# First gate on TensorE, sines on GpSimd, softmax division on ScalarE: one change to a two-layer network kernel

## The chip, the core and the metric

The kernel runs on one core of one Trainium2 chip. The metric is the device time of one launch in microseconds (us). The kernel before takes 1743.57 us (median of three runs, 1743.54 to 1747.07).

The engines are called as in the profile: PE is TensorE, PEld its weight loads, DVE is VectorE, ACT is ScalarE, POOL is GpSimd, SP is SyncE, which here issues every DMA. Each engine runs its own list of instructions in order and waits on semaphores of the others.

## The reference

A sequence of 256 tokens with 1024 channels goes through four mixers (latent attention "MLA", a state space mixer "S5", a gated linear recurrence, block attention) and MLPs. Each layer is modulated by a vector `c`: `silu(c) @ w + b` is cut in three 1024-wide thirds, shift, scale and gate. Only the start of the network is touched by the change:

```
def modulation(cs, w, b):
    m = cs @ w + b
    shift, scale, gate = jnp.split(m, 3, axis=-1)

z = h @ w_in                                   # 1024 -> 256 + 128 + 64
cq  = rms_norm(z[..., :256], q_norm)
ckv = rms_norm(z[..., 256:384], kv_norm)
k_pe = apply_rope(z[..., 384:], cos, sin)
q  = cq @ w_qb                                 # 8 heads of 128 + 64
kv = ckv @ w_kvb                               # 8 heads of 128 + 128
p = softmax(where(causal, (qn kn^T + qp k_pe^T) * scale, -1e30))
o = (p @ v) @ w_o
```

The S5 mixer also needs tables of powers of its complex decay (products of sines and cosines of `li * dt * 2^e`), which do not depend on the tokens and are built early.

## The kernel before, in words

All big weights come from one list of 512 KB units, `UNITS`, made by `plan()`. SP loads them in that order into 7 raw buffers. Unit kinds: `w` is a weight that ACT copies to a rounded high part (`wh`, L454) and DVE (`wl`, L460) or POOL (L458) subtracts to a low part, both into a ring of 11 slots; `p` is an MLA weight used as it is, in a slot of the ring that has not been needed yet (`early`); `m` is a modulation unit, 128 columns of a third, for which DVE multiplies the unit with `silu(c)` and sums along the row (one SCALAR_TENSOR_TENSOR of 128x1024 and a short read of the sum, L508). `run(maxn)` takes the next units of the list in order wherever it is called; what it emits stands on DVE, ACT and POOL at that place of the program. A raw buffer is free, and the load seven units further on can start, when the unit's instruction has read it.

Order of the work up to the first MLP, as the code writes it:

- setup: `silu(c)`, decay powers on POOL, then the sines on DVE (`sincos`, L894 to L903), the rotary tables by POOL copies (L975 to L984) and PE transposes (L989).
- `mla`: eight pairs of modulation units (shift and scale of the first layer), each followed by the modulation of 128 channels of the transposed input and the PE product with `mla_in`; then the squares of the latents on ACT (L1071), the power -1/2 on POOL (`rpow`, L635), the normalised latents, their transposes on PE (`turn_z`, L1098), the keys (`kvk`), values (`kvv`) and first query pair (`q_pair`).
- `heads`: eight heads in a software pipeline of letters. S is the scores on PE, B the maximum on DVE, E the exponentials on ACT, N the reciprocal and the division by the sum on DVE (L1210), T the transposes on PE (L1024) with an ACT copy (L1025), A the product with the values; `q` makes the next query pair, a digit calls `run` with that many units, `t` issues background work (the four stores of the recurrence tables, `tab_d`, L1334, which wait for POOL).
- Inside the heads, `run` passes modulation units to DVE: the rest of the second modulation and the eight units of the first layer's gate (`mod02`). When the gate's sums are done, `modfin` is set: `mod_finish` turns the column into rows with 16 PE instructions against the identity (L392 with `gcol`), and while it is pending inside the heads no further modulation unit is taken.
- `mla_o` boundary: output projection in two halves of tokens; for each half a layer norm on DVE (`ln_part`, L651 to L666, with `rpow` on POOL), transposes on PE, the modulated transposed input `z` (L623) and its split `xh`, `xl` (L590).
- MLP 0: the first weights (`mlp0.f`) are used in two passes, one for each half of the tokens; their results leave the banks by a DVE copy (L848), one for each pass, and PE transposes them.

From the second of these two copies on, the two kernels issue the same instructions in the same order on every engine.

Of the kernel before, what the change touches and what calls it, by code (L numbers as in the profile page):

```python
# [38 lines left out]
HEADS0 = "T2 S0 B0 1 A2 E0 N0 t q t 1"  # L39
# [3 lines left out]
ROT = 0  # L43
G0 = 1
GSTEP = 2.0
ROT_T = 21.5
ROT_U = 6.0
# [41 lines left out]
MODS_AT = 8  # L89
# [7 lines left out]
def plan():  # L97
# [4 lines left out]
    m = _mod(1, 0) + _mod(1, 1) + _mod(0, 2)  # L102
# [23 lines left out]
def _unit(inp, kind, tag, k, out):  # L126
# [6 lines left out]
    if kind == "m":  # L133
        i, third = int(tag[3]), int(tag[4])
        nm, l = _MOD[i]
        o = 1024 * third + 128 * k
        out[:] = inp[nm + "_w"][l][:, o:o + 128].T
        return
# [62 lines left out]
def _cols_spec():  # L201
    s = [("dsk", lambda i: i["ssm_d"][0])]
# [112 lines left out]
class Model:  # L315
    def __init__(self, ctx, tc, ws, cols, rows, x, pos, inv, rel, sp, sbc, sgb, out):
# [9 lines left out]
        slot = lambda j: sb.tile([128, 1024], F32, name="early%d" % j, tag="w%s%d" % ("hl"[j % 2], RING - 1 - j // 2))  # L326
        self.pt = {u: slot(6 + j) for j, u in enumerate(PUNITS)}
        self.early = [slot(j) for j in range(6)]
        self.rt, self.nop, self.opdone = [], 0, set()
        self.XH, self.XL = T("xh", [128, 8, 256], F32R), T("xl", [128, 8, 256], F32R)  # L330
# [16 lines left out]
        self.mhalf = T("mhalf", [128, 4])  # L347
        self.lri = T("lri", [128, 8], I32)
# [16 lines left out]
        self.fill = 0  # L365

# [56 lines left out]
    def run(self, look=LOOK, maxn=99, mods=2):  # L423
        n = 0
        while self.nproc < len(UNITS) and n < maxn:
# [13 lines left out]
            if u[0] == "w":  # L439
# [6 lines left out]
                if own is None and s >= RING - 3 and self.early:  # L446
                    break
# [50 lines left out]
    def mod_unit(self, u, raw):  # L498
        nc, tag, k = self.nc, u[1], u[2]
        i, third = int(tag[3]), int(tag[4])  # L500
        if k == 0:
            self.mod_finish()
# [12 lines left out]
        if k == 7:  # L515
            if third < 2:
                nc.vector.tensor_tensor(self.mcol[i][third], self.msum, self.col("modb%d" % i, 8 * third, 8), op=OP.add)
                self.mods.add(tag)
            else:
                nc.vector.tensor_tensor(self.gcol, self.msum, self.col("modb%d" % i, 16, 8), op=OP.add)  # L520
                nc.vector.tensor_scalar(self.gcol, self.gcol, 1.0, None, op0=OP.add)
                self.modfin = [tag, 3]
# [365 lines left out]
    def sincos(self, s, c, ang, t1, t2):  # L888
        nc = self.nc
        tau = 2.0 * math.pi  # L890
# [3 lines left out]
        nc.vector.tensor_scalar(t1, ang, 1.0 / tau, MAGIC, op0=OP.mult, op1=OP.add)  # L894
        nc.vector.tensor_scalar(t1, t1, -MAGIC, None, op0=OP.add)
        nc.vector.scalar_tensor_tensor(t2, t1, -c1, ang, op0=OP.mult, op1=OP.add)
        nc.vector.scalar_tensor_tensor(t2, t1, -c2, t2, op0=OP.mult, op1=OP.add)
        nc.vector.scalar_tensor_tensor(t2, t1, -c3, t2, op0=OP.mult, op1=OP.add)
        nc.vector.tensor_scalar(t2, t2, 3.1415925, -3.1415925, op0=OP.min, op1=OP.max)
        nc.scalar.activation(s, t2, func=AF.Sin)  # L900
        nc.scalar.activation(t1, t2, func=AF.Sin, scale=0.5)
        nc.vector.scalar_tensor_tensor(t1, t1, -2.0, t1, op0=OP.mult, op1=OP.mult)
        nc.vector.tensor_scalar(c, t1, 1.0, None, op0=OP.add)  # L903
# [21 lines left out]
    def setup(self):  # L925
# [3 lines left out]
        spt = self.Z[1][:, 1664:1664 + NSP]  # L929
        inv = self.Z[1][:, 1600:1632]  # L930
# [12 lines left out]
        V.memset(self.mhalf, -0.5)  # L943
        jp = self.Z[0][:, 0:128]
# [12 lines left out]
        self.rel(*cb)  # L957
        self.ssm_decay(spt, pi)
        while self.nproc < 2:
            self.step()  # L960
        V.tensor_copy(self.identb, self.ident)
        V.tensor_copy(self.maskb, self.mask)
        posf = self.stat(2)
        V.tensor_copy(posf, posi)
        n = 64 + 7 * 32
        a, t1, t2 = (self.Z[1][:, n * i:n * i + n] for i in range(3))
        sc = self.Z[1][:, 3 * n:5 * n].rearrange("p (e a) -> p e a", e=2)
        for h in range(2):
            V.tensor_scalar(a[:, 32 * h:32 * h + 32], inv, posf[:, h:h + 1], None, op0=OP.mult)
        for e in range(7):  # L970
            V.tensor_scalar(a[:, 64 + 32 * e:96 + 32 * e], self.sw[2], float(1 << (e + 1)) if e else 1.0, None, op0=OP.mult)
        self.sincos(sc[:, 0], sc[:, 1], a, t1, t2)
        self.tok = self.sb.tile([128, 2, 2, 32], F32, name="tok")
        for e in range(2):
            G.tensor_copy(self.tok[:, e], sc[:, 1 - e, 0:64].rearrange("p (h f) -> p h f", h=2))  # L975
        CT, ST = self.B2, self.BR
        for h in range(2):
            for j in range(4):
                o = slice(128 * h + 32 * j, 128 * h + 32 * j + 32)
                G.tensor_copy(CT[:, o], self.tok[:, 0, h])  # L980
                if j % 2 == 0:
                    G.tensor_scalar(ST[:, o], self.tok[:, 1, h], -1.0, None, op0=OP.mult)
                else:
                    G.tensor_copy(ST[:, o], self.tok[:, 1, h])  # L984
        self.ssm_powers(sc[:, 1, 64:], sc[:, 0, 64:])
# [54 lines left out]
    def mla(self):  # L1040
# [4 lines left out]
        gen = self.ssm_inputs()  # L1045
        next(gen)
        xb = [self.pair_transposes(self.X, 2 * i) for i in range(4)]
        zb = [self.bank(), self.bank()]
        for k in range(8):
# [13 lines left out]
            if k % 2:  # L1063
                self.done(u)
                self.rel(xb[k // 2])
        ZT = self.B2
# [9 lines left out]
        next(gen)  # L1076
        for half in range(2):
            z, o = zb[half], ZT[:, 512 * half:512 * half + 512]
            c, s = self.tok[:, 0, half], self.tok[:, 1, half]
# [14 lines left out]
        for j in (2, 0, 1, 3):  # L1094
# [926 lines left out]
```

## Time and profile before

| quantity | value |
|---|---|
| median of three runs | 1743.57 us |
| profiled execution, its own time | 1742.75 us |
| its span, first to last instruction | 1740.9 us |
| mean granted TensorE clock | 0.956 |
| PE busy | 1602.5 us (92%) |
| DVE busy | 1157.7 us (67%) |
| ACT busy | 833.7 us (48%) |
| POOL busy | 508.8 us (29%) |

The profile shows one execution of the program. The terms of the sum are taken from it and set against its own time. [...] `fp32r` in a shape is the rounded type of the split weights; the `mla` products are plain fp32, for which the trace shows two loads and two MATMUL rows for one product.

### The profile page before, as it was taken

Reading aid. Unit: us, or ns where it says so; the run is one execution under the profiler, and the core shown is the slowest. Engines: PE = TensorE matmul, PEld = TensorE weight load, DVE = VectorE, ACT = ScalarE, POOL = GpSimd, SP = SyncE. Lnnn points to the kernel's source line nnn. Section 1 sums busy time; section 2 is a strip of 40 time slices with the busy share of each in tenths; the row PEclk is TensorE's granted clock in tenths of the full one; section 3 lists DMA queues with packets and bytes.
Section 4 is the critical chain, followed back from the end, with each engine's and each line's share of the span. In section 5 each row is a group of like instructions: output and inputs, shape, how many; then the busy total and the mean of one; then the engine's idle time right before and its main releaser. Section 6 shows DMA issues by size and latency. Waiting matters only on the chain. (4 is left out here: it accounts for less than half of the span.)

```text
span 1740.9 us, 25278 instructions
## 1 busy us (share of the span) xinstructions
PE 1602.5 (92%) x9690; PEld 1417.2 (81%) x9690; DVE 1157.7 (67%) x1480; ACT 833.7 (48%) x1252; POOL 508.8 (29%) x557
## 2 busy tenths in 40 slices
PE   4778999998789999999999759999999999999998
PEld 2557798887677899789998747999899999779997
DVE  6688986578978655776556787555656554765553
ACT  2343656555345655354445735444544443754441
POOL 8945699608848100100004441000000001230000
PEclk9869999898889999999999879999999999999999
DMA  9477678767556666466554336565455664536640
GB/s 365 172 279 256 226 248 281 273 243 263 220 170 222 239 229 212 152 219 225 176 181 134 118 121 217 176 239 173 137 188 214 213 211 133 182 133 207 214 149 25
DMA packets 106588, 349.64 MB, mean 201 GB/s; under 512 B 12385, under 2 KB 22753, under 8 KB 106466
## 3 DMA queue, kind: packets, MB, share of 16 engines
q1 hardware_dynamic: 106466, 348.02, 57.7%
q8 instruction: 76, 1.25, 0.3%
q14 instruction: 46, 0.38, 0.1%
HBM read 338.40 MB, written 9.57 MB: 200 GB/s over the span
## 5 line engine op out<-in xcount | busy, mean ns | idle before, releaser
L460 DVE TENSOR_TENSOR wl<-raw,wh 128x1024 fp32r<-128x1024 f32 x445 | 562.7, 1298 | 193.1 <-ACT wh L454 191.7
L454 ACT ACTIVATE wh<-raw 128x1024 fp32r<-128x1024 f32 x484 | 490.3, 1051 | 275.1 <-PE bank L392 140.9
L392 PE MATMUL bank<-xh,wh 128*128 128x256 f32 x1728 | 490.1, 284 | 0.0
L392 PE MATMUL bank<-xh,wl 128*128 128x256 f32 x1728 | 489.7, 283 | 0.0
L392 PE MATMUL bank<-xl,wh 128*128 128x256 f32 x1728 | 489.1, 283 | 0.0
L392 PEld LDWEIGHTS bank<-xh,wh 128*128 128x128 f32 x1728 | 330.6, 191 | 2.4 <-issue 0.2
L392 PEld LDWEIGHTS bank<-xl,wh 128*128 128x128 f32 x1728 | 330.5, 191 | 2.1
L392 PEld LDWEIGHTS bank<-xh,wl 128*128 128x128 f32 x1728 | 330.5, 191 | 0.0
L392 PE MATMUL bank<-wh,hh 128*128 128x512 f32 x736 | 297.4, 404 | 24.8 <-ACT hh L1827 23.8
L392 PE MATMUL bank<-wl,hh 128*128 128x512 f32 x736 | 294.5, 400 | 2.8 <-POOL wl L458 2.8
L392 PE MATMUL bank<-wh,hl 128*128 128x512 f32 x736 | 244.8, 398 | 4.2 <-DVE hl L590 2.0
L635 POOL TENSOR_TENSOR st<-st,mhalf 128x1 f32<-128x1 f32 (+1 forms) x33 | 21.9, 664 | 694.8 <-DVE st L643 608.1
L458 POOL TENSOR_TENSOR wl<-raw,wh 128x256 fp32r<-128x256 f32 x156 | 156.7, 1037 | 138.0 <-ACT wh L454 129.8
L392 PEld LDWEIGHTS bank<-wh,hh 128*128 128x128 f32 x736 | 142.0, 193 | 55.9 <-ACT hh L1827 25.3
L392 PEld LDWEIGHTS bank<-wh,hl 128*128 128x128 f32 x736 | 141.1, 192 | 37.5 <-DVE hl L590 2.9
L392 PEld LDWEIGHTS bank<-wl,hh 128*128 128x128 f32 x736 | 142.2, 193 | 33.1 <-POOL wl L458 5.0
L508 DVE SCALAR_TENSOR_TENSOR junk<-raw,cs 128x1024 bf16<-128x1024 f32 x96 | 138.0, 1437 | 18.3 <-DMA raw<-in_ws_dram 17.1
L392 PE MATMUL bank<-wl,xh 128*128 128x512 f32 x320 | 126.6, 396 | 1.9 <-DVE wl L460 1.0
L392 PE MATMUL bank<-wh,xh 128*128 128x512 f32 x320 | 127.4, 398 | 0.7 <-ACT wh L454 0.7
L590 DVE TENSOR_TENSOR hl<-z,hh 128x512 fp32r<-128x512 f32 x72 | 52.5, 731 | 95.5 <-ACT hh L589 95.3
L392 PE MATMUL bank<-wh,xl 128*128 128x512 f32 x320 | 102.0, 396 | 6.5 <-DVE xl L590 6.4
L589 ACT ACTIVATE hh<-z 128x512 fp32r<-128x512 f32 x72 | 45.5, 632 | 116.4 <-DVE z L875 104.4
(389 smaller groups left out, 1807.2 us busy)
## 6 DMA issues: line engine op xcount, KB each, us to landing
raw<-in_ws_dram SPq DMA_DIRECT2D x580, 512.0 KB
early<-in_ws_dram SPq DMA_DIRECT2D x10, 512.0 KB
grow<-in_rows_dram SPq DMA_DIRECT2D x9, 512.0 KB
brow<-in_rows_dram SPq DMA_DIRECT2D x6, 512.0 KB
ophh<-ops_d SPq DMA_DIRECT2D x6, 512.0 KB
ophl<-ops_d SPq DMA_DIRECT2D x6, 512.0 KB
gate<-in_rows_dram SPq DMA_DIRECT2D x5, 512.0 KB
tab_d<-early SPq DMA_DIRECT2D x4, 512.0 KB
```

The source lines that it names most:

```text
L392: self.nc.tensor.matmul(out, l, r, start=start, stop=stop)
L454: self.nc.scalar.activation(self.Hs[s], raw, func=AF.Copy)
L458: self.nc.gpsimd.tensor_tensor(self.Ls[s][:, w], raw[:, w], self.f32(self.Hs[s])[:, w], op=OP.subtract)
L460: self.nc.vector.tensor_tensor(self.Ls[s], raw, self.f32(self.Hs[s]), op=OP.subtract)
L508: nc.vector.scalar_tensor_tensor(self.junk, raw, 1.0, self.cs, op0=OP.mult, op1=OP.mult, accum_out=total)
L589: self.nc.scalar.activation(hdst, src, func=AF.Copy)
L590: self.nc.vector.tensor_tensor(ldst, src, self.f32(hdst), op=OP.subtract)
L635: self.nc.gpsimd.tensor_tensor(r, v, self.mhalf[:, 0:n], op=OP.pow)
```

## The change

Six things are done.

1. The eight units of the first gate are stored by rows and multiplied on PE: for each unit, eight 128x128 blocks are loaded as weights and one column of `silu(c)` is streamed (`pe_unit`). In the list they come before the second modulation's units.
2. The sines are made by POOL and two ACT lookups; the rotary tables by ACT copies. The first five steps of the first recurrence table (`rotations`) now stand on POOL ahead of the `rpow` of the latents, the decay powers (`ssm_powers`) and the rest behind it.
3. The division by the softmax sum is an ACT copy with a scale. The recurrence tables are stored after the heads.
4. Modulation units `m[0:5]` and `m[5]` of the second modulation are handled before the heads, the other ten come between the units of `mla_o`.
5. The small decay tables (`ssm_tables`) are turned and stored in the first layer norm of the boundary.
6. The first seven units of `MODS0` move from ahead of `mlp0.f[3]` to behind `mlp0.f[7]`.

```diff
+HEADS0 = "T2 S0 B0 A2 E0 1 N0 q 1"
-HEADS0 = "T2 S0 B0 1 A2 E0 N0 t q t 1"
...
-    for k, (a, b) in enumerate(((0, 0), (0, 2), (2, 4), (4, 24))):
-        o += [("p", "qb", k)] + m[a:b]
-    o += _w("mla_o", 8)
+    m, g, w = _mod(1, 0) + _mod(1, 1), _mod(0, 2), _w("mla_o", 8)
+    o += g[:4] + m[:5] + [("p", "qb", 0)] + g[4:] + m[5:9] + [("p", "qb", k) for k in (1, 2, 3)]
+    for k in range(8):
+        o += [w[k]] + m[9 + k:10 + k]
     m = _ffn_order("mlp0", N_FF, 8, False)
-    o += m[:3] + MODS0[:MODS_PRE] + _weave(m[3:], MODS0[MODS_PRE:], MODS_AT)
+    o += m[:8] + MODS0[:MODS_PRE] + _weave(m[8:], MODS0[MODS_PRE:], MODS_AT)
...
+    def pe_unit(self, tag, k, raw):
+        if k == 0:
+            self.pbk = self.bank()
+        for j in range(8):
+            self.mm(self.pbk[:, j:j + 1], raw[:, 128 * j:128 * j + 128], self.cst[:, k:k + 1],
+                    k == 0 and j == 0, k == 7 and j == 7)
...
-        nc.vector.scalar_tensor_tensor(t2, t1, -c1, ang, op0=OP.mult, op1=OP.add)
...
+        for x in (c1, c2, c3):
+            G.tensor_scalar(t2, t1, -x, None, op0=OP.mult)
+            G.tensor_tensor(ang, ang, t2, op=OP.add)
...
         r = self.rpow(ss, 4)
-        next(gen)
+        self.rotations(0, range(5, 6))
+        self.rotations(1, range(6))
+        self.ssm_powers()
+        self.run(maxn=4, mods=4)
...
+        turn_z((2, 0, 1))
...
-                nc.vector.tensor_scalar(P[h % 3][:, w], P[h % 3][:, w], rc[:, i:i + 1], None, op0=OP.mult)
+                if bias is None:
+                    nc.scalar.activation(P[h % 3][:, w], P[h % 3][:, w], func=AF.Copy, scale=rc[:, i:i + 1])
```

Three places show what this does to the order. The first is PE between the last `mla_in` product and the first query pair; before, the transposes (L1098), keys (`early_74`), values (`early_75`), the small table (L1316) and the queries (`early_76`) follow one another.

```order
L1098 MATMUL bank_125<-ident,b2row 128x128
L1098 MATMUL bank_126<-ident,b2row 128x128
L392 MATMUL bank_127<-gate,early_74 128x256 x2
L392 MATMUL bank_128<-gate,early_74 128x256 x2
L392 MATMUL bank_129<-gate,early_74 128x256 x2
L392 MATMUL bank_130<-gate,early_74 128x256 x2
L392 MATMUL bank_131<-early_75,gate 128x512
L392 MATMUL bank_124<-early_75,gate 128x512
L392 MATMUL bank_125<-early_75,gate 128x512
L392 MATMUL bank_126<-early_75,gate 128x512
L1316 MATMUL bank_127<-ident,grow 128x128 x2
L392 MATMUL bank_128<-gate,early_76 128x256 x4
```

The same stretch after, from the third gate unit on; a row with `cst,raw` is one gate unit.

```order
L401 MATMUL bank_125<-cst,raw_67 128x1 x8
L401 MATMUL bank_125<-cst,raw_68 128x1 x8
L401 MATMUL bank_128<-gate,early_74 128x256 x2
L401 MATMUL bank_124<-gate,early_74 128x256 x2
L401 MATMUL bank_129<-gate,early_74 128x256 x2
L401 MATMUL bank_130<-gate,early_74 128x256 x2
L1157 MATMUL bank_126<-ident,b2row 128x128
L1157 MATMUL bank_127<-ident,b2row 128x128
L401 MATMUL bank_125<-cst,raw_67 128x1 x8
L401 MATMUL bank_131<-early_75,gate 128x512
L401 MATMUL bank_128<-early_75,gate 128x512
L401 MATMUL bank_124<-early_75,gate 128x512
```

One gate unit stands ahead of the transposes, three between them and the keys, one between keys and values and three between values and queries; the small table is gone from here.

The second place is DVE behind the eight heads. Before, from the last but one `hl` (the low part of a head's output) on: only splits (L460), the three modulation columns and, at the end, two modulation units (L508) stand ahead of the layer norm (L651).

```order
L590 TENSOR_TENSOR hl_89<-bank_128,hh_88 128x256
L460 TENSOR_TENSOR wl_55_848<-raw_66,wh_55_847 128x1024
L1005 SCALAR_TENSOR_TENSOR scol<-mc_112,cols 128x8
L1006 SCALAR_TENSOR_TENSOR bcol<-mc_112,cols 128x8
L1007 TENSOR_TENSOR bcol<-bcol,mc_111 128x8
L460 TENSOR_TENSOR wl_56_866<-raw_67,wh_56_865 128x1024
L460 TENSOR_TENSOR wl_57_871<-raw_68,wh_57_870 128x1024
L460 TENSOR_TENSOR wl_58_924<-raw_69,wh_58_923 128x1024
L460 TENSOR_TENSOR wl_59_929<-raw_63,wh_59_928 128x1024
L460 TENSOR_TENSOR wl_60_934<-raw_64,wh_60_933 128x1024
L508 SCALAR_TENSOR_TENSOR junk,msum<-raw_65,cs 128x1024
L508 SCALAR_TENSOR_TENSOR junk,msum<-raw_66,cs 128x1024
```

After, a part of the same stretch, where the units (L520) and the splits (L469) alternate.

```order
L520 SCALAR_TENSOR_TENSOR junk,msum<-raw_67,cs 128x1024
L469 TENSOR_TENSOR wl_43_854<-raw_68,wh_43_853 128x1024
L520 SCALAR_TENSOR_TENSOR junk,msum<-raw_69,cs 128x1024
L469 TENSOR_TENSOR wl_45_861<-raw_63,wh_45_860 128x1024
L520 SCALAR_TENSOR_TENSOR junk,msum<-raw_64,cs 128x1024
L469 TENSOR_TENSOR wl_47_868<-raw_65,wh_47_867 128x1024
L520 SCALAR_TENSOR_TENSOR junk,msum<-raw_66,cs 128x1024
L469 TENSOR_TENSOR wl_49_875<-raw_67,wh_49_874 128x1024
```

Behind the last `hl` there are now ten units and eleven splits ahead of the layer norm; inside the heads there is neither.

The third place is DVE between the two copies of MLP 0. Before, five units stood ahead of the first `z` of the boundary (L623), and behind the first copy came splits at once.

```order
L508 SCALAR_TENSOR_TENSOR junk,msum<-raw_64,cs 128x1024
L623 TENSOR_SCALAR z_100<-bank_128,scol,bcol 128x128 x4
...
L848 COPY z_98<-bank_125 128x512
L460 TENSOR_TENSOR wl_55_848<-raw_63,wh_55_847 128x1024
L460 TENSOR_TENSOR wl_56_866<-raw_64,wh_56_865 128x1024
```

After, seven units stand between the first copy (L880) and the same splits.

```order
L880 COPY z_96<-bank_125 128x512
L520 SCALAR_TENSOR_TENSOR junk,msum<-raw_63,cs 128x1024
L520 SCALAR_TENSOR_TENSOR junk,msum<-raw_64,cs 128x1024
L520 SCALAR_TENSOR_TENSOR junk,msum<-raw_65,cs 128x1024
L520 SCALAR_TENSOR_TENSOR junk,msum<-raw_66,cs 128x1024
L520 SCALAR_TENSOR_TENSOR junk,msum<-raw_67,cs 128x1024
L520 SCALAR_TENSOR_TENSOR junk,msum<-raw_68,cs 128x1024
L520 SCALAR_TENSOR_TENSOR junk,msum<-raw_69,cs 128x1024
L469 TENSOR_TENSOR wl_53_889<-raw_63,wh_53_888 128x1024
```

Ahead of the boundary's first `z` there is now one split and no unit.

## Rows read from the trace of the kernel before

**Rows 1.** Windows: stretch, length, busy us and count per engine, clock, DMA, GB/s

```profile
20.00:40.00 20.00, 10.99 (x35) 7.59 (x36) 16.14 (x37) 4.56 (x9) 19.45 (x38) 1.00 1.03 409
51.00:57.00 6.00, 4.43 (x13) 2.92 (x14) 4.17 (x9) 2.25 (x7) 5.33 (x17) 0.50 0.04 13
...
128.00:131.00 3.00, 3.00 (x15) 2.91 (x15) 2.38 (x4) 1.83 (x4) 0.00 (x0) 0.50 0.86 309
```

**Rows 2.** Timeline of DVE, modulations and latents: start, us, instruction, [idle before <-releaser]

```profile
17.11 1.22 DVE L508 SCALAR_TENSOR_TENSOR junk<-raw,cs 128x1024 bf16<-128x1024 f32 x1
...
36.94 0.15 DVE L1055 TENSOR_TENSOR bcol<-msum,cols 128x1 f32<-128x1 f32 x1
47.40 0.17 DVE L1073 TENSOR_SCALAR st<-st 128x2 f32<-128x2 f32 x1 [10.31 <-ACT junka L1071]
```

**Rows 3.** Timeline of POOL around the power of the latents

```profile
50.19 1.03 POOL L635 TENSOR_TENSOR st<-st,mhalf 128x4 f32<-128x4 f32 x1
...
51.38 0.41 POOL L1333 TENSOR_TENSOR early<-early,spp 128x16 f32<-128x16 f32 x2
...
54.74 2.45 POOL L1333 TENSOR_TENSOR early<-early,spp 128x64 f32<-128x64 f32 x2
```

**Rows 4.** Timeline of PE from the latents to the first queries

```profile
33.59 13.11 PE L392 MATMUL bank<-early,z 128*128 128x448 f32 x32
51.68 0.73 PE L1098 MATMUL bank<-ident,b2row 128*128 128x128 f32 x2 [4.98 <-ACT b2row L1089]
...
55.20 5.66 PE L392 MATMUL bank<-gate,early 128*128 128x256 f32 x16
...
64.35 3.62 PE L392 MATMUL bank<-gate,early 128*128 128x256 f32 x16
```

**Rows 5.** Timeline of PE, heads and the gate's rows

```profile
105.50 0.49 PE L1024 MATMUL bank<-ident,z 128*128 128x128 f32 x3
...
108.61 0.49 PE L1024 MATMUL bank<-ident,z 128*128 128x128 f32 x3
...
115.15 0.90 PE L1024 MATMUL bank<-ident,z 128*128 128x128 f32 x3 [2.85 <-DVE z L1210]
...
120.93 0.85 PE L1024 MATMUL bank<-ident,z 128*128 128x128 f32 x3
...
127.18 1.65 PE L392 MATMUL bank<-z,z 128*128 128x256 f32 x4 [1.16 <-ACT z L1025]
128.62 3.09 PE L392 MATMUL bank<-ident,gcol 128*128 128x128 f32 x16
```

**Rows 6.** Waits of SP from 60 to 130: total us, times, longest

```profile
SPq L1334 <- POOL early L1333: 33.6, 4, 15.5
```

**Rows 7.** Timeline of DVE from the last head to the boundary's first z

```profile
129.28 0.42 DVE L590 TENSOR_TENSOR hl<-bank,hh 128x256 fp32r<-128x256 f32 x1
...
133.33 5.77 DVE L460 TENSOR_TENSOR wl<-raw,wh 128x1024 fp32r<-128x1024 f32 x5 [1.52 <-ACT wh L454]
...
142.53 0.69 DVE L651 TENSOR_TENSOR r<-bank,gate 128x512 f32<-128x512 f32 x1 [1.02 <-PE bank L392]
...
157.98 1.36 DVE L623 TENSOR_SCALAR z<-bank,scol,bcol 128x128 f32<-128x128 f32 x4
```

**Rows 8.** Timeline of PE, the two stalls behind the boundary

```profile
159.99 1.22 PE L392 MATMUL bank<-wh,xl 128*128 128x512 f32 x2 [4.47 <-DVE xl L590]
...
195.62 1.57 PE L856 MATMUL bank<-ident,z 128*128 128x128 f32 x7 [4.20 <-DVE z L848]
```

**Rows 9.** Timeline of DVE between the two copies of MLP 0

```profile
174.62 0.68 DVE L848 COPY z<-bank 128x512 f32<-128x512 f32 x1
175.22 9.62 DVE L460 TENSOR_TENSOR wl<-raw,wh 128x1024 fp32r<-128x1024 f32 x6
184.76 1.76 DVE L508 SCALAR_TENSOR_TENSOR junk<-raw,cs 128x1024 bf16<-128x1024 f32 x1
...
194.89 0.68 DVE L848 COPY z<-bank 128x512 f32<-128x512 f32 x1
```

More of the change, by code (lines that the diff above doesn't have):

```diff
@@ L88 @@
 MODS0 = _mod(2, 0) + _mod(2, 1) + _mod(1, 2)
-MODS_AT = 8
+MODS_AT = 3
+ROWMODS = {'mod02'}
 MODS_PRE = 7
@@ L135, in _unit @@
         nm, l = _MOD[i]
+        if tag in ROWMODS:
+            rows(inp[nm + "_w"][l], slice(1024 * third, 1024 * third + 1024))
+            return
         o = 1024 * third + 128 * k
@@ L347, in __init__ @@
         self.mhalf = T("mhalf", [128, 4])
+        self.one, self.cst = T("one", [128, 1]), T("cst", [128, 8])
+        self.pbk = None
         self.lri = T("lri", [128, 8], I32)
@@ L365, in __init__, with halves @@
         self.fill = 0
+    def halves(self):
+        self.XH, self.XL = (self.sb.tile([128, 8, 256], F32R, name=t, tag=t) for t in ("xh", "xl"))
     def hidden(self, i):
@@ L445, in run @@
                     break
-                if own is None and s >= RING - 3 and self.early:
+                if own is None and not self.lent.get(s, set()) <= self.finished:
                     break
@@ L500, in mod_unit @@
         i, third = int(tag[3]), int(tag[4])
+        if tag in ROWMODS:
+            self.pe_unit(tag, k, raw)
+            return
         if k == 0:
@@ L943, in setup @@
         V.memset(self.mhalf, -0.5)
+        V.memset(self.one, 1.0)
         jp = self.Z[0][:, 0:128]
@@ L985, in setup @@
-        self.ssm_powers(sc[:, 1, 64:], sc[:, 0, 64:])
+            nc.scalar.activation(a[:, 64 + 32 * e:96 + 32 * e], self.sw[2], func=AF.Copy, scale=float(1 << (e + 1)) if e else 1.0)
+        gen = self.sincos(sc[:, 0], sc[:, 1], a, t1, t2)
+        next(gen)
+        yield
+        next(gen)
+        self.tok = [[sc[:, 1 - e, 32 * h:32 * h + 32] for h in range(2)] for e in range(2)]
+        self.cosn, self.sinn = sc[:, 1, 64:], sc[:, 0, 64:]
+        nc.scalar.activation(self.Ec, self.cosn[:, 32:224], func=AF.Copy)
@@ L1044, in mla @@
         XT = self.Z[2].rearrange("p (k t) -> p k t", k=8)
-        gen = self.ssm_inputs()
-        next(gen)
+        ang = self.angles()
+        next(ang)
         xb = [self.pair_transposes(self.X, 2 * i) for i in range(4)]
@@ L1065, in mla @@
                 self.rel(xb[k // 2])
+            if k in (3, 5):
+                next(ang)
+        V.tensor_copy(self.identb, self.ident)
+        V.tensor_copy(self.maskb, self.mask)
         ZT = self.B2
@@ L1093, in mla, with turn_z @@
         tb = [self.bank(), self.bank()]
-        for j in (2, 0, 1, 3):
+        def turn_z(js):
+            for j in js:
+                for half in range(2):
+                    nc.tensor.transpose(tb[half][:, 128 * j:128 * j + 128],
+                                        ZT[:, 512 * half + 128 * j:512 * half + 128 * j + 128], self.ident)
+        turn_z((2, 0, 1))
+        for j in (2, 0, 1):
             for half in range(2):
@@ L1116, in mla @@
         self.done(u)
+        turn_z((3,))
+        for half in range(2):
+            nc.scalar.activation(KP[:, 128 * half:128 * half + 128], tb[half][:, 384:512], func=Copy)
+        self.rel(*tb)
         self.run(maxn=5, mods=5)
@@ L1236, in ssm_decay @@
         self.spt = spt
-        w = self.sw = [self.Z[0][:, 128 + 32 * i:160 + 32 * i] for i in range(24)]
+        w = self.sw = [self.wide[0][:, 32 * i:32 * i + 32] for i in range(24)]
         self.apr = sp[:, 0:160].rearrange("p (q d) -> p q d", d=5)
@@ L1358, in store, with put_tables @@
+    def put_tables(self):
+        for b in range(2):
             for e in range(2):
                 d = self.tab_d[2 * b:2 * b + 2, :, 512 * e:512 * e + 512].rearrange("b p n -> p b n")
-                dma(d, tabs[b][e].rearrange("p (b n) -> p b n", b=2))
-        rotations(0, range(ROT))
-        yield 0.0
-        rotations(0, range(ROT, 6))
-        rotations(1, range(6))
-        yield ROT_T
-        store(0)
-        yield ROT_U
-        store(1)
-        self.early = None
+                self.nc.sync.dma_start(out=d, in_=self.tabs[b][e].rearrange("p (b n) -> p b n", b=2))
+        self.finished.add("tables")
```

176 lines of the change are left out of this document (92 added, 84 removed).

## The prediction

> **What bounds the kernel now.** I read the table by windows first, to find the stretches in which PE is not the limit, then the timeline of each engine there, then the same stretch in the order of the changed kernel. Behind the second copy of MLP 0 (194.89 [rows 9]) both kernels issue the same instructions, and PE waits for that copy (4.20 us at 195.62 [rows 8]). So the question is when that copy ends; what it gains or loses, the whole rest, which PE bounds, is taken to gain or lose too. Up to there the limit changes hands four times:
>
> - Until 37 it is the stream of weights: 409 GB/s at a DMA share of 1.03 [rows 1], with DVE taking the units in order until 36.94 [rows 2].
> - From 46.70, the end of the last product with `mla_in` (33.59 + 13.11 [rows 4]), PE waits for the power of the latents. The last squares come at 47.40 [rows 2], but POOL gets to the power only at 50.19, 1.03 long, behind the decay powers [rows 3]. The transposes start at 51.68, the keys at 55.20, at a granted clock of 0.50 until 57 [rows 1, 4]; the first queries end at 67.97 (64.35 + 3.62 [rows 4]).
> - The heads run from there to 128.83 (127.18 + 1.65 [rows 5]), 60.9 us. From one T to the next it takes 3.11 us where DVE is in time (105.50 to 108.61) and 5.8 (115.15 to 120.93) or more where a unit stands ahead of the division and PE waits for it, as 2.85 us at 115.15 [rows 5]. SP stands 33.6 us in all in front of the table stores [rows 6], and loads behind them come late.
> - Then DVE: 13.25 us from the last `hl` to the layer norm (129.28 to 142.53), 15.45 to the first `z` at 157.98 with five units in it [rows 7], a PE stall of 4.47 us [rows 8], and 20.3 us between the two copies (174.62 to 194.89), filled with DVE work [rows 9].
>
> **The change, part by part.** Base: the profiled execution's 1742.75 us, its span of 1740.9 and 1.85 around it; the median of the runs is 0.8 above, so what is worked out holds for either.
>
> *Latents.* The sine leaves DVE, where the units begin again only at 17.11 [rows 2], but the stream caps what is won: I put the last unit at 35.3 instead of 36.94 (an estimate) and the squares at 40. The power then waits for POOL alone, which now has eleven sine operations, two of them behind ACT, and the thirty of five rotation steps ahead of it. Beside a stream of units on DVE a POOL operation takes 1.22 us (2.45 for two of 128x64), beside nothing about 0.2 (0.41 for two of 128x16) [rows 3]. Sine: 11 x 1.22 and some 3.5 us of ACT lookups and waits, from about 11 to 28. Until 35.3 five rotation operations at 1.22; then twenty-five with no price in a row for the larger ones: between 0.2 (5 us) and 1.22 (30 us). I take 0.42, near the quiet rows since DVE has stopped, with the shapes growing to 128x256: 10.5, so 45.8. With 1.03 the power is out at 46.9 instead of 51.2: **-4.3** (ends -8 and +15; I keep -8 and +4, since with DVE silent 1.22 has no cause).
>
> *Gate on PE.* Removed: eight DVE units of 1.22, in the heads. Added: 64 products, 16 rows a unit. One unit is hidden ahead of the transposes, seven stand between `rpow` and the first scores with nothing else for PE to do. The nearest row is the gate's own rows against the identity: 16 rows in 3.09 us [rows 5] at a clock of 0.50 [rows 1], and half of it, 1.55, if the same work runs at 1.00. Bounds 1.55 and 3.1 a unit; I take 2.5, since PE has been idle for ten microseconds ahead and such a wait left it at 0.50 from 51 to 57 [rows 1]. 7 x 2.5 = **+17.5** (10.9 to 21.7). The keys gain, since PE is no longer fresh from a wait: 5.66 against 3.62 for the queries' sixteen rows [rows 4], of which I take **-1.3**. The loads for units 5 to 8 wait for PE, but the stream is near idle there (share 0.04 [rows 1]) and one load is covered by keys or values. The first scores so start 11.9 late, at about 79.9.
>
> [...] The row gives 0.193 us a load (3.09 / 16 [rows 5]) at 0.50 [rows 1]. [...] No run here shows such a unit at full clock yet.
>
> *Heads.* DVE loses units and splits in the heads altogether, because the gate's `modfin` is pending all through them, and the division goes to ACT, which has room. SP is no longer stopped. So PE's own period holds: eight of 3.11 = 24.9 [rows 5], three query pairs of 3.62 = 10.9 [rows 4], and about 5 us for the last head to leave the pipeline: 41 us (38 with that tail hidden, 48 with the clock at 0.50 in a part) against 60.9: **-20**. The last product ends near 120.7, **8.0 early** in all.
>
> *Behind the heads.* What was spread over the heads is now in one queue: behind the last `hl` ten units and eleven splits. At 1.22 and a little for the sum's read, 1.27 x 10 = 12.7 [rows 2]; 11 splits at 1.15 to 1.23 (5.77 for five [rows 7]) = 13.1; column operations and the small table's additions 1.7; 0.4 for `hl`: 27.9 against 13.25, **+14.6**. PE went through its first half beside the 13.25 us of before, and so is not the limit in 27.9. The layer norm starts **6.6 late**. With seven raw buffers full, fourteen loads and four stores, 18 of 0.52 MB in 27 us, ask for 350 GB/s, under the 409 of [rows 1] but near enough for 0 to +3.
>
> *Boundary.* The five units ahead of `z` go, up to 1.76 each [rows 9], and with them most of the 4.47 us stall and some 2 us of slow matmuls behind it (0.61 each at 159.99 [rows 8]). From the start of the norm to `xl` it took 17.5 us (142.53 to 159.99); less five units, plus one split and the wait for the transposes it takes about 11.5. PE ran dry 13.0 us after the norm's start (159.99 - 4.47 - 142.53), but now the norm starts about 3 us behind PE's first half, so PE still waits some 2 us; and the second norm's power stands behind all POOL splits of `mlp0.f`. Net **-5** at the first copy (-6.5 to -1), so +1.6 there.
>
> *Between the copies.* The seven units stand here now, nine units and ten splits in all. While POOL finishes the residual, a DVE operation takes 1.6 (9.62 for six [rows 9]); POOL has eleven operations left, so eleven of nineteen at 1.69 and eight at 1.22, with the column and the copy some 29 us against 20.3: **+8.7** (7 x 1.22 without contention gives +8.5, less if splits get cheaper with POOL done: +5; 7 x 1.76 gives +12).
>
> [...] Rows 9 have a unit at 1.76 beside POOL where [rows 2] have 1.22. [...]
>
> Sum: -4.3 + 17.5 - 1.3 - 20 + 14.6 - 5 + 8.7 = **+10.2**, so 1742.75 + 10.2 = **1753 us**.
>
> **The rivals.**
>
> *A, the gate is cheap, faster.* PE takes a unit at full clock, 1.55: -6.6 against my sum. With the power out at 44 (-3) and the heads at 38 (-3) the sum is -2.4, and -6.1 with +5 between the copies: 1737 to 1740. For it: once PE is busy it gets faster (0.50 at 51 to 57 [rows 1], the queries in 3.62 at 64.35 [rows 4]). Against: it needs nearly every term at its good end; it decides from a unit under 1.6 together with a layer norm less than 1 us late. Chance 0.17. [...]
>
> *B, half clock throughout.* Loads with one column leave PE at 0.50: 3.1 a unit (+4.2), keys, values and queries at half (5.66 against 3.62, twice, +4), the first heads at 5.8 instead of 3.11 for three of them (+8): +26, 1769; with part of it, 1763 to 1769. For it: 0.50 in 128 to 131, during just such loads [rows 1]. Against: the heads kept 3.11 wherever PE had no wait [rows 5]. Chance 0.2.
>
> *C, absorbed.* The late start only empties other waits, so that the second copy is no later: for instance units and splits pass while PE waits anyway. For it: PE waits in front of both copies' consumers [rows 8]. Against: it waits for DVE, whose queue has grown by what was moved. 1741 to 1746, chance 0.13.
>
> *D, the stream paces the stretch behind the heads* (+3) and POOL's splits the second norm: 1757; within my range.
>
> **How the numbers follow.** Forecast with D 0.5: 1747 to 1761, likeliest 1753. A 0.17, B 0.2, C 0.13. A measurement can tell 0.2%, 3.5 us, from no change. C and a small part of A fall within it: same 0.15; faster 0.15; slower 0.7. The range reaches into A and B: 1739 to 1767.
>
> **What would show it.** `turn_z` from about 47 and the first scores near 80; sixteen rows of a gate unit in 2.5 us; a period near 3.1 in the heads and no DVE unit in them; the last head at 121, the layer norm at 149, no 4.47 us stall, the second copy at about 205, and from there the same distances as before. The forecast is wrong if the first scores start before 73 or after 86, if DVE's queue behind the heads takes under 24 us, or if the distance to the end changes behind the second copy.

## The result, and the profile after

The changed kernel takes 1763.66 us (median of four runs, 1761.1 to 1765.75) against 1744.28 for the kernel before beside it: a ratio of 1.0107, 95% interval 1.0089 to 1.0126, so 19.4 us slower. Forecast were 1753 (1739 to 1767) and slower, 10 us more than before: the side is right, the size is about half of what was measured. The profiled execution of the changed kernel has a span of 1759.3 us, 18.4 more than before. Executions of one kernel differ by several us (the kernel before ran between 1742.1 and 1751.3 beside the run gate_out), so times are compared by all runs, and a trace is one execution.

The timeline of PE from the end of the latents to the first scores answers to [rows 4] and the first half of [rows 5] (start, us, instruction, idle time before it and what ended it). `cst,raw` is the gate, sixteen rows a unit.

```profile
40.84 1.84 PE L401 MATMUL bank<-cst,raw 128*128 128x1 f32 x16
47.75 1.81 PE L1157 MATMUL bank<-ident,b2row 128*128 128x128 f32 x6 [5.07 <-ACT b2row L1148]
49.35 10.24 PE L401 MATMUL bank<-cst,raw 128*128 128x1 f32 x48
59.45 5.20 PE L401 MATMUL bank<-gate,early 128*128 128x256 f32 x16
64.49 0.38 PE L1157 MATMUL bank<-ident,b2row 128*128 128x128 f32 x2
64.71 1.84 PE L401 MATMUL bank<-cst,raw 128*128 128x1 f32 x16
66.42 3.68 PE L401 MATMUL bank<-early,gate 128*128 128x512 f32 x8
69.93 7.66 PE L401 MATMUL bank<-cst,raw 128*128 128x1 f32 x48
77.46 6.42 PE L401 MATMUL bank<-gate,early 128*128 128x256 f32 x16
83.72 0.59 PE L401 MATMUL bank<-r,z 128*128 128x256 f32 x2
```

The first scores start 15.9 us late. Three units ahead of the keys take 3.4 us each, one 1.7, the last three 2.5 each, and the queries behind them 6.42 instead of 3.62 [rows 4]. The windows of the same stretch (as [rows 1]: length, busy time of PE, PEld, DVE, ACT and POOL, then the granted clock) say why:

```profile
49.30:59.50 10.20, 10.20 (x51) 10.20 (x49) 9.67 (x13) 0.88 (x3) 9.85 (x10) 0.50 0.44 156
...
66.50:70.00 3.50, 3.50 (x11) 1.59 (x10) 0.00 (x0) 1.79 (x3) 3.26 (x6) 1.00 0.99 377
70.00:77.50 7.50, 7.50 (x50) 7.50 (x48) 0.00 (x0) 0.60 (x1) 7.11 (x8) 0.68 1.02 385
77.50:83.70 6.20, 6.20 (x17) 5.04 (x18) 1.49 (x4) 0.60 (x1) 6.12 (x3) 0.56 1.02 363
83.70:124.00 40.30, 35.35 (x178) 25.58 (x177) 13.74 (x42) 20.92 (x65) 15.94 (x70) 1.00 0.05 19
```

PE shows as busy through all of it, and yet its clock stays at 0.50 for ten microseconds of gate units and falls from 1.00 to 0.68 and 0.56 in and behind the last three. The unit at full clock (1.00 in 64.5 to 66.5) takes 1.71 us to the start of what follows (64.71 to 66.42); at that price seven would take 12.0, they took 19.3, and the queries 2.8 more than before, so the half clock cost about 10 us here (an estimate from these rows). In the heads, from 83.7 to 124, the clock is 1.00. Then DVE, from the last `hl` on; the rows answer to [rows 7] and [rows 9]:

```profile
127.65 0.42 DVE L622 TENSOR_TENSOR hl<-bank,hh 128x256 fp32r<-128x256 f32 x1 [2.44 <-ACT hh L621]
127.99 1.22 DVE L520 SCALAR_TENSOR_TENSOR junk<-raw,cs 128x1024 bf16<-128x1024 f32 x1
...
155.39 0.68 DVE L683 TENSOR_TENSOR r<-bank,gate 128x512 f32<-128x512 f32 x1
...
164.10 1.35 DVE L655 TENSOR_SCALAR z<-bank,scol,bcol 128x128 f32<-128x128 f32 x4
...
180.78 0.68 DVE L880 COPY z<-bank 128x512 f32<-128x512 f32 x1
181.38 1.21 DVE L520 SCALAR_TENSOR_TENSOR junk<-raw,cs 128x1024 bf16<-128x1024 f32 x1
182.52 0.07 DVE L520 DVE_READ_ACCUMULATOR junk<-raw,cs 128x1 f32 x1
182.63 1.64 DVE L520 SCALAR_TENSOR_TENSOR junk<-raw,cs 128x1024 bf16<-128x1024 f32 x1
...
192.61 10.13 DVE L469 TENSOR_TENSOR wl<-raw,wh 128x1024 fp32r<-128x1024 f32 x6
...
210.62 0.68 DVE L880 COPY z<-bank 128x512 f32<-128x512 f32 x1
```

27.7 us from the last `hl` to the layer norm, 25.4 to the first copy, 29.8 to the second. Six marks, read in this way in every kernel of this study, tell where each is early or late (us; the span is from the first to the last instruction). Each row is one execution, so a few us in its last column decide nothing:

| kernel | first scores | last head ends | layer norm | first copy | second copy | span |
|---|---|---|---|---|---|---|
| before | 67.81 | 128.83 | 142.53 | 174.62 | 194.89 | 1740.9 |
| after | 83.72 | 127.20 | 155.39 | 180.78 | 210.62 | 1759.3 |
| gate_out | 63.55 | 110.77 | 138.99 | 163.85 | 194.22 | 1743.3 |
| gate_wide | 79.73 | 123.83 | 152.13 | 178.38 | 208.22 | 1757.3 |
| gate_dve | 64.24 | 116.64 | 145.57 | 171.27 | 201.13 | 1749.6 |
| norm_dve | 84.21 | 123.10 | 151.22 | 176.95 | 206.78 | 1755.9 |
| b_norm_act | 68.40 | 131.91 | 146.24 | 178.49 | 198.78 | 1750.6 |
| inheads | 84.20 | 142.63 | 161.59 | 187.58 | 217.43 | 1763.8 |
| m0early | 83.95 | 127.54 | 158.70 | 189.33 | 209.60 | 1759.8 |
| after_post | 84.43 | 127.67 | 155.56 | 181.64 | 198.54 | 1755.1 |
| late | 61.70 | 126.12 | 141.26 | 166.12 | 196.49 | 1745.7 |
| late_m0 | 63.35 | 127.27 | 145.06 | 177.10 | 197.38 | 1748.1 |
| late_post | 60.77 | 125.21 | 140.68 | 165.54 | 182.96 | 1739.8 |
| b_post | 66.79 | 130.54 | 144.03 | 168.93 | 186.34 | 1742.6 |
| dve_heads2 | 76.24 | 129.64 | 147.55 | 173.26 | 203.09 | 1754.5 |

### The profile page after: what moved, and what is told of

Read it like the earlier page. It is cut to its first block, busy times and chain, and to the rows that moved or that the text cites. A ratio compares the mean times of both kernels' runs of the same rounds, so it can differ in the third digit from the quotient of the medians.

```text
span 1759.3 us, 25519 instructions
## 1 busy us (share of the span) xinstructions
PE 1618.5 (92%) x9818; PEld 1428.5 (81%) x9818; DVE 1135.4 (65%) x1434; ACT 844.0 (48%) x1286; POOL 497.5 (28%) x548
## 5 line engine op out<-in xcount | busy, mean ns | idle before, releaser
L469 DVE TENSOR_TENSOR wl<-raw,wh 128x1024 fp32r<-128x1024 f32 x445 | 561.2, 1294 | 194.8 <-ACT wh L463 193.4
L467 POOL TENSOR_TENSOR wl<-raw,wh 128x256 fp32r<-128x256 f32 x156 | 153.1, 1016 | 134.7 <-ACT wh L463 134.0
L520 DVE SCALAR_TENSOR_TENSOR junk<-raw,cs 128x1024 bf16<-128x1024 f32 x88 | 128.5, 1461 | 11.7 <-DMA raw<-in_ws_dram 10.5
```

What stands on the lines that cost most here:

```text
L467: self.nc.gpsimd.tensor_tensor(self.Ls[s][:, w], raw[:, w], self.f32(self.Hs[s])[:, w], op=OP.subtract)
L469: self.nc.vector.tensor_tensor(self.Ls[s], raw, self.f32(self.Hs[s]), op=OP.subtract)
L520: nc.vector.scalar_tensor_tensor(self.junk, raw, 1.0, self.cs, op0=OP.mult, op1=OP.mult, accum_out=total)
```

## The experiments

The theory after the result: the gate's products stand in the path for some 20 us, because PE takes most of them at a clock of 0.50 to 0.68 and pays for it in the queries too (0.56); the shorter heads give most of it back, and the work of DVE that left the heads costs again what it took there. Rivals: the shorter heads come from ACT as divider; the place of DVE's units alone makes the loss. Theories A and B below are, for each run, those of its own expectation. Ratios are against the kernel before beside the run, with 95% intervals.

**gate_out.** Products of seven of the gate's units left out.

```diff
-        for j in range(8):
+        for j in range(8 if k == 0 else 0):
...
-                    k == 0 and j == 0, k == 7 and j == 7)
+                    j == 0, j == 7)
```

> The changed kernel with the products of gate units 1 to 7 left out (unit 0 alone is multiplied, so the gate is not the reference's); loads and order stay. Theory A (the gate's rows on PE stand in the path at about 19 us and keep the clock low for the first queries): the queries in 3.6 instead of 6.4 us, first scores at 63 to 65 instead of 83.7, the time 18 to 22 us less, about 1743. Theory B (the gate is only one of many small losses, and what is won ahead of the heads is lost again in a wait behind them): first scores early by as much, but the time only 5 to 10 us less.

Measured: ratio 0.9992 (0.9979 to 1.0004), 1745.2 us against 1746.6. The first scores come at 63.55, the queries take 3.62. The timeline of PE:

```profile
50.64 5.97 PE L401 MATMUL bank<-gate,early 128*128 128x256 f32 x16 [0.46 <-ACT gate L1166]
...
60.10 3.62 PE L401 MATMUL bank<-gate,early 128*128 128x256 f32 x16
63.55 0.59 PE L401 MATMUL bank<-r,z 128*128 128x256 f32 x2
...
68.10 5.41 PE L401 MATMUL bank<-gate,early 128*128 128x256 f32 x16 [1.23 <-DMA early<-in_ws_dram]
```

Theory A holds: 20.2 us at the first scores, 16.4 to 16.9 at the marks from the last head to the second copy, 16.0 in the span; by the medians 18.5. Some of the 20.2 is lost again in the heads (47.2 us against 43.5), where the second queries wait for their weights and take 5.41 us. The gate's products are the whole loss; without their price the rest of the change is even, though its other parts were not tried one by one.

**gate_wide.** The same products, each with its column streamed 64 times. The run asks whether the clock of 0.50 in 49.3 to 59.5, and of 0.68 and 0.56 in 70 to 83.7, goes with the one column behind each load or with the waits around.

```diff
-            self.mm(self.pbk[:, j:j + 1], raw[:, 128 * j:128 * j + 128], self.cst[:, k:k + 1],
+            self.mm(self.pbk[:, 64 * j:64 * j + 64], raw[:, 128 * j:128 * j + 128], self.cst[:, k:k + 1].to_broadcast([128, 64]),
...
-            nc.vector.tensor_tensor(dst, self.pbk[:, 0:8], self.col("modb%d" % i, 8 * third, 8), op=OP.add)
+            nc.vector.tensor_tensor(dst, self.pbk[:, 0:512:64], self.col("modb%d" % i, 8 * third, 8), op=OP.add)
```

> The changed kernel with the same column of silu(c) streamed 64 times for each block of the gate instead of once; results, loads and order stay, each product only has more columns. [...]

Measured: ratio 1.0077 (1.0061 to 1.0093). The windows, and the timeline of PE:

```profile
49.30:59.50 10.20, 10.20 (x50) 10.20 (x49) 9.76 (x13) 0.89 (x3) 9.77 (x11) 0.50 0.41 156
...
70.00:77.50 7.50, 7.50 (x57) 6.83 (x56) 1.04 (x2) 1.19 (x2) 7.11 (x8) 1.00 0.98 347
```

```profile
49.41 10.34 PE L401 MATMUL bank<-cst,raw 128*128 128x64 f32 x48
59.54 6.10 PE L401 MATMUL bank<-gate,early 128*128 128x256 f32 x16
...
70.92 5.47 PE L401 MATMUL bank<-cst,raw 128*128 128x64 f32 x48
76.22 3.67 PE L401 MATMUL bank<-gate,early 128*128 128x256 f32 x16
```

The clock goes with the columns, but only in the last three units. These begin at full clock and now keep it (1.00 in 70 to 77.5, where it was 0.68): 5.47 us instead of 7.66 though they stream 64 times as much, and the queries fall from 6.42 to 3.67. The first three, which begin at 0.50, stay there as before (0.50, 10.34 us). In norm_dve, m0early, inheads and after_post, with one column again, the queries behind the last three units take 6.2 to 6.7 us, so the 3.67 is no accident of one trace. The first scores come 4.0 us earlier than in the changed kernel: so much of the loss goes with the columns. What held the first three at 0.50 is not shown; they follow a wait of PE in both kernels (5.07 us in the changed one, 5.79 here).

**gate_dve.** The gate back on DVE, at the same place in the list.

```diff
-ROWMODS = {'mod02'}
+ROWMODS = set()
...
```

> The changed kernel with the gate back on DVE, at the same place of the list. PE loses seven units of 1.7 to 3.4 us, DVE gains seven of 1.22 to 1.7 in front of the first queries' rotation. Theory A: DVE needs 18 us for fourteen units from about 50, PE is ready by 63, first scores complete at 69 to 73 instead of 85, so 12 to 15 us less in the end, about 1750. Theory B: POOL's table steps slow every unit to 1.7, DVE is no better than PE, first scores at 77 or later, and the time within 5 us of the changed kernel.

Measured: ratio 1.0045 (1.003 to 1.006), 1754.2 us, 9 to 11 less than the changed kernel: a little under A's 12 to 15. PE is ready at 64.24 but then waits 6.96 us, to 71.80, for the rotated queries, which stand behind thirteen units on DVE (the first four, from 51.1 to 58.8, at 1.6 to 2.2 us, the others at 1.2); the last head ends at 116.6.

**norm_dve and b_norm_act.** The division alone: back to DVE in the changed kernel, and to ACT in the kernel before.

```diff
-                if bias is None:
-                    nc.scalar.activation(P[h % 3][:, w], P[h % 3][:, w], func=AF.Copy, scale=rc[:, i:i + 1])
-                else:
-                    nc.vector.tensor_scalar(P[h % 3][:, w], P[h % 3][:, w], rc[:, i:i + 1], None, op0=OP.mult)
+                nc.vector.tensor_scalar(P[h % 3][:, w], P[h % 3][:, w], rc[:, i:i + 1], None, op0=OP.mult)
```

The edit of norm_dve is shown; that of b_norm_act is its reverse.

> The changed kernel with the division by the softmax sum back on DVE. Theory A (the heads got shorter because no unit, no split and no blocked store is left in them; which engine divides does not matter): the heads 43 to 46 us as before this edit (43.5), the time within 3 us. Theory B (ACT as divider is what shortened them): the heads 50 us or more, the time 6 us or more above the changed kernel's.

> The kernel before with the division by the softmax sum on ACT, nothing else changed. Theory A (the units of DVE ahead of the reciprocal and the loads that SP issues late hold the heads; the division itself is a small part): the heads 55 to 59 us instead of 61.0, the time 2 to 6 us less, 1738 to 1742 where the kernel before takes 1744. Theory B (the division on DVE is the main stop of the heads): the heads below 52 us, the time 9 or more less. Third: the order of ACT's queue makes every head wait and the time is the same or more.

Measured: norm_dve 1.0075 (1.006 to 1.0091), heads 38.9 us instead of 43.5; b_norm_act 1.0019 (1.0006 to 1.0032), heads 63.5 instead of 61.0. In the changed kernel the division on ACT makes the heads longer (43.2 to 44.1 in after, gate_wide, m0early and after_post, which have it alike); neither case of norm_dve had that. In the kernel before it does not make them shorter, so A and B of b_norm_act fall, and by the time its third case came. That it makes them longer there is not shown: in b_post the same instructions up to there, with the division on DVE, take 63.8. Of the gain in the heads ACT has no part. ACT in the changed kernel, one head:

```profile
114.86 0.80 ACT L1278 ACTIVATE z<-z,st 128x256 f32<-128x256 f32 x2 [0.23 <-DVE st L1275]
115.56 0.47 ACT L1077 ACTIVATE z<-bank 128x384 f32<-128x384 f32 x1
```

and PE, first of the changed kernel, then with the division on DVE (T to T, and A):

```profile
113.24 0.49 PE L1076 MATMUL bank<-ident,z 128*128 128x128 f32 x3
...
116.08 0.92 PE L401 MATMUL bank<-z,z 128*128 128x256 f32 x4 [0.28 <-ACT z L1077]
116.84 0.49 PE L1076 MATMUL bank<-ident,z 128*128 128x128 f32 x3
```

```profile
112.25 0.49 PE L1076 MATMUL bank<-ident,z 128*128 128x128 f32 x3
114.65 0.87 PE L401 MATMUL bank<-z,z 128*128 128x256 f32 x4
115.36 0.49 PE L1076 MATMUL bank<-ident,z 128*128 128x128 f32 x3
```

ACT's copy of the transposed exponentials (L1077), for which A waits, stands behind a division that itself waits for the reciprocal: 3.60 us from T to T. On DVE the division is in nobody's way: 3.11, PE's own period of [rows 5].

**inheads.** The ten units and the eight splits let into the heads.

```diff
-                if mods == 0 or (self.hold and self.modfin is not None):
+                if mods == 0 or (self.hold and self.modfin is not None and u[1] not in ("mod10", "mod11")):
...
-        if k == 0:
+        if k == 0 and not (self.hold and tag == "mod11"):
             self.mod_finish()
```

> The changed kernel with the ten units of the second modulation and the eight splits of the output projection allowed inside the heads, though the gate's column is ready. Theory A (the queue of DVE behind the heads is what makes the layer norm late): from the last low part to the layer norm 15 to 17 us instead of 27.7, the heads longer by 0 to 5, the time 8 to 12 us less, 1752 to 1756. Theory B (the units in the heads stop PE as they did before the change, so the place does not matter): the heads longer by 10 or more and the time within 4 us of the changed kernel's 1763.

Measured: ratio 1.0126 (1.0105 to 1.0146). Theory B came: behind the last `hl` 9.2 us are won (18.5 to the layer norm), but the heads take 58.4 instead of 43.5. DVE and PE in them:

```profile
108.06 1.23 DVE L469 TENSOR_TENSOR wl<-raw,wh 128x1024 fp32r<-128x1024 f32 x1 [1.33 <-ACT wh L463]
109.20 0.16 DVE L1275 RECIPROCAL st<-st 128x2 f32<-128x2 f32 x1
```

```profile
110.68 1.65 PE L401 MATMUL bank<-z,z 128*128 128x256 f32 x4 [2.42 <-ACT z L1077]
```

The reciprocal stands behind a split that waits for ACT, and ACT's division behind the reciprocal: two queues in turn, 6.5 us a head.

**m0early and after_post.** The seven units of MLP 0 back at the boundary (first edit), and behind both copies (second edit).

```diff
-MODS_AT = 3
+MODS_AT = 8
...
-    o += m[:8] + MODS0[:MODS_PRE] + _weave(m[8:], MODS0[MODS_PRE:], MODS_AT)
+    o += m[:3] + MODS0[:MODS_PRE] + _weave(m[3:], MODS0[MODS_PRE:], MODS_AT)
```

```diff
-MODS_AT = 3
+MODS_AT = 10
...
-MODS_PRE = 7
+MODS_PRE = 0
```

> The changed kernel with the seven units back where they were, two ahead of the first layer norm and five ahead of the first z, none between the copies. Theory A (the place of the seven units only shifts the wait): norm 2.5 us later, norm to first copy back from 25.4 to about 32, copy to copy back from 29.8 to about 20, the sum within 3 us: 1761 to 1766. Theory B (the move itself made the kernel slower, since PE hides the units at the boundary but not between the copies): 6 to 10 us less, 1753 to 1757.

> The changed kernel with the seven units of MLP 0 behind both copies in the same way, all else as in the change. Theory A (the sixth part of the change alone costs 8.7 us between the copies): copy to copy 20 to 21 us instead of 29.8, the time 7 to 10 us less, 1752 to 1756. Theory B (the gain is given back behind): 1760 or more.

Measured: m0early 1.0081 (1.0065 to 1.0097), after_post 1.0091 (1.0068 to 1.0114). In m0early norm to copy is 30.6 and copy to copy 20.3, as A had it, with the norm 3.3 later: the second copy moves by 1.0 only. In the time about 4 us are left, between A and B; the intervals of m0early and of the changed kernel overlap, so even that is not clear. In after_post copy to copy is 16.9 and the second copy 12.1 us earlier, but the time, 1762.9 us, is the changed kernel's: theory B, the gain is given back behind. (Its trace is of an execution of 1756.95 us, well under that median.)

**b_post.** The same move in the kernel before (`MODS_PRE = 0`, `MODS_AT = 15`).

> The kernel before with the seven units taken from the boundary to behind both copies. Theory A (five units and the 4.47 us stall go, the norm comes 2.5 us earlier or not at all): the first z 8 to 11 us earlier, the second copy at 184 to 190, the time 1734 to 1740. Theory B (the stretch behind the copies takes it back): 1743 or more. In both the offset against the kernel before between 285 and 390 us tells whether PE's extra wait there, seen in every run with other code ahead, comes with any shift or with this change's code.

Measured: ratio 1.0011 (1.0 to 1.0022), again B: the second copy 8.6 us earlier and nothing of it in the time. Against the trace of the kernel before, PE is 9.3 us ahead at 250, 2.5 at 262 and 2.8 behind at 287. PE and DVE there:

```profile
254.99 1.05 PE L392 MATMUL bank<-z,b2row 128*128 128x128 f32 x4 [4.91 <-DVE b2row L1476]
```

```profile
246.94 1.75 DVE L460 TENSOR_TENSOR wl<-raw,wh 128x1024 fp32r<-128x1024 f32 x1 [4.52 <-ACT wh L454]
...
279.43 1.80 DVE L460 TENSOR_TENSOR wl<-raw,wh 128x1024 fp32r<-128x1024 f32 x1 [8.79 <-ACT wh L454]
```

DVE waits there for weights that come late, while POOL is busy for 71 to 98% of every ten microseconds from 230 to 300, with the S5 operators. SP, which issues the loads, waits for these operators too: 10.9 us from 230 to 290 here, 13.3 in the kernel before. What comes early to this stretch waits in it; that POOL is what paces it is not shown.

**dve_heads2, late_m0, late and late_post.** Versions put together from these runs. dve_heads2 has the gate on DVE and units and splits in the heads (edits of gate_dve and inheads, and another order of the units); its list lets the gate's rows be written over the input of the queries, so that part is not the reference's, and these rows now stand ahead of the values on PE. In late_m0, late and late_post the list of before is back, but the gate's eight units, 64 columns each, fall into the heads on PE; the division is on DVE, and in the heads a unit stands ahead of A again; they differ in the place of the seven units (at the boundary, between the copies, behind both). The edit of the list of these three:

```diff
-    o += g[:4] + m[:5] + [("p", "qb", 0)] + g[4:] + m[5:9] + [("p", "qb", k) for k in (1, 2, 3)]
-    for k in range(8):
-        o += [w[k]] + m[9 + k:10 + k]
+    m = m + g
+    for k, (a, b) in enumerate(((0, 0), (0, 2), (2, 4), (4, 24))):
+        o += [("p", "qb", k)] + m[a:b]
+    o += w
```

> The changed kernel with the gate back on DVE, its eight units and four of the second modulation ahead of the heads, the other twelve and the splits inside the heads. Theory A (PE loses what the gate's products took, and DVE's queue behind the heads is gone): first scores at 64, heads 48 to 56, layer norm at 130 to 138 instead of 155 (before: 142.5), the time 1735 to 1742, a little under the kernel before. Theory B (units and splits in the heads stretch them, as in the run with both let in, to more than 60): layer norm at 142 or later and the time 1747 or more.

> A version built from the runs so far: the changed kernel with the list of before (second modulation first, its sixteen units on DVE; the gate's eight units last), so that the gate's products fall into the heads on PE, 64 columns each, with the division on DVE, a unit of the list ahead of A and one behind q as before, and the seven units of MLP 0 back at the boundary. Theory A (in the heads of before PE is idle for a quarter and DVE is the limit, so products on PE there cost less than units on DVE): first scores complete at 68 to 72, heads 48 to 56, layer norm at 132 to 139 against 142.5 in the kernel before, the time 1734 to 1742, below the kernel before. Theory B (PE has no room in the heads either, since they follow PE's own chain): heads 60 or more, the time 1745 or more.

> As the run late_m0, but with the seven units of MLP 0 between the copies as in the changed kernel. Theory A (where the seven stand only moves the wait): within 3 us of late_m0. Theory B (between the copies nothing covers them): 4 to 8 us above late_m0.

> As the run late, but the seven units of MLP 0 are behind both copies, spread over the rest of MLP 0 with the others. Theory A (behind the second copy DVE has room, since PE bounds there, so the 30 us between the copies fall to about 20 and nothing comes back): second copy at 186 to 190, the time 6 to 10 us under late, 1738 to 1743, at or below the kernel before. Theory B (the units are late for the stretch behind, where PE then waits for DVE or for loads): the second copy as early, but the time 1746 or more.

Measured: dve_heads2 1.0069 (1.0055 to 1.0084), with 6.14 us of PE waiting for the gate's column in front of the values, so that the first scores come at 76 and not at 64; late_m0 1.0026 (1.0012 to 1.0041), theory B; late 1.0037 (1.0024 to 1.005), within 3 us of late_m0, theory A; late_post 1.001 (1.0 to 1.0021), 1747.2 us, theory B. The expected 1734 to 1742 did not come. In the heads PE was not as free as thought: with the gate in them and the first scores at 61.70 they take 64 us. late_post has its second copy 11.9 us before that of the kernel before and gives this back in the same stretch: 12.7 ahead at 250, 0.3 behind at 287. (Its trace is of an execution of 1741.58 us, under its median.) Against late, whose second copy is 13.5 us later, 3 to 5 us are kept. No version beats the kernel before.

## Why the side was right and the size was not

The span grew by 18.4 where the terms gave 10.2. Of the 8.2 between them, 3.6 are the gate on PE, 2.5 the heads and 2.7 the stretch behind the second copy; the others nearly cancel. Term by term, by the marks:

- *Latents*, forecast -4.3, measured -3.9 (power out at 47.29 against 51.22 [rows 3]). The later rotations ahead of it, with DVE busy for 3.7 of the 10.75 us from 35.5 to 46.25, ran near the price taken (0.45 us each against 0.42).
- *Gate on PE*, forecast +17.5 and -1.3 for the keys. From the power to the first scores it was 19.8 more: units +19.3, keys -0.5, queries +2.8, transposes and small table -1.9. This is the step that failed, in two ways. The queries behind the gate's units had no term, as if they kept their 3.62; they took 6.42 at a clock of 0.56. And the keys were said to gain because PE is "no longer fresh from a wait": PE had been busy for ten microseconds and still stood at 0.50. I had read a busy PE as one that speeds up. The units themselves took 2.76 us on average against 2.5. It was luck that the miss is no larger: the transposes and the small table, which had no term, gave back 1.9. gate_wide takes 4.0 us of the price away by columns alone, and gate_out shows the whole, 16 us in the span and 18.5 by the medians.
- *Heads*, forecast -20 (41 us), measured -17.5 (43.5). "The division goes to ACT, which has room" failed: ACT has room, but not at that place of its queue. norm_dve gives 38.9.
- *Behind the heads*, forecast +14.6, measured +14.5 (28.2 from the last head's end to the norm against 13.7). The term was right. inheads then shows that the other place was no better: the same work inside the heads costs more than it saves behind them (14.9 us against 9.2).
- *Boundary*, forecast -5, measured -6.7; *between the copies*, forecast +8.7, measured +9.6. One edit, net +2.9 against +3.7. Six of the seven units took 1.64 us while POOL was busy (9.76 of the 10 us from 182.6 to 192.6); the row read for it has 1.76.
- *Behind the second copy* the forecast had nothing: "the whole rest is taken to gain or lose too". It was +15.7 at the copy and +18.4 at the end. Between 275 and 387 us PE falls 3 to 8 us further behind the one trace of before in each of the eleven kernels that leave the seven units ahead of the second copy, b_norm_act too (+3.8 at 275, +7.2 at 387); most then catch up a part. All of this leans on that one trace: gate_out is 2.4 us later than it in the span, but not later by the runs (0.9992). So that some 3 us are lost here is not shown. What after_post, b_post and late_post do show is that a gain of 9 to 14 us at the second copy is for the most part gone at 287; what in that stretch takes it stays open.

Of the rivals, B (half clock) named the clock, and the time it gave, 1763 to 1769, holds the result, but in part by luck. The queries slowed as it said (6.42). Its units at 3.1 took 2.76 on average, keys and values took 5.20 and 3.68, about as before, and the heads, from which it had +8, ran at 1.00. Nor did its row bear on it: the sixteen rows of 128 to 131 [rows 1] are the `ident,gcol` of [rows 5], which stream 128 columns each, and the clock had been 0.50 all through 115 to 128, where PE waits again and again (busy for 9.73 of 13.0 us). The kernel before has no product of one column, so no row of it could show what such loads do to the clock.

A unit at full clock, which no row of the kernel before has, took 1.84 us for its sixteen rows at 64.71 (clock 1.00); the three that begin at 0.50 took 3.4 each.

What the forecast said would show it: first scores near 80 (84), a period of 3.1 (3.60), the last head at 121 (127), layer norm at 149 (155), second copy at 205 (211), no 4.47 us stall (none). The distance behind the second copy, which was not to change, grew by 2.7 in the two traces.

## What to carry to other kernels

Work moved to an engine that looked idle was paid here at the place in that engine's queue where it landed: price what stands behind it (the queries behind the gate, 6.42 us instead of 3.62; ACT's copy behind the division, 3.60 us from T to T against 3.11), not only the work itself. When PE is to do a kind of product that the kernel has nowhere yet, no row prices it: run it alone once, and read the granted clock beside its time. And before a gain of some microseconds is carried to the end, look for a later stretch with another bound, which may keep it.

## What the runs showed of the hardware

In the changed kernel TensorE's granted clock fell while PE showed no idle time: 1.00 in 66.5 to 70, 0.68 in 70 to 77.5 and 0.56 in 77.5 to 83.7, in and behind three gate units with one column a load. With 64 columns a load (gate_wide) the same stretch stayed at 1.00. Ahead of the keys, where PE came out of a wait of 5.07 us (5.79 in gate_wide), 48 rows of such loads stayed at 0.50 for 10.2 us with either number of columns; the clock was 0.70 in 59.5 to 64.5, with the keys (0.51 in gate_wide), and 1.00 in 64.5 to 66.5. PE and PEld both show 10.20 of 10.20 us as busy at 0.50, and 2.00 of 2.00 at 1.00 in 64.5 to 66.5: here the busy share did not tell the clock. Sixteen rows of a unit took 1.71 us at 1.00 and 3.4 at 0.50.
